# A two-layer hybrid decoder trunk on one core: padding the SBUF tiles to multiples of 256 bytes

## Chip, cores and metric

The kernel runs on one core of one Trainium2 chip. The metric is the device time of one execution in microseconds (us). Three runs of the kernel before took 1142.94, 1142.59 and 1142.89 us; the median is 1142.89.

## What is computed

One sequence of 512 tokens with 1024 channels (float32) goes through two layers, each with an RMS norm, an input projection, two mixers with SiLU gates, an output projection and a residual add; a last RMS norm follows. Cut to its shape:

```
def even_layer(x, ...):
    z = rmsnorm(x, norm_g) @ w_in                       # 1024 -> 5120
    a, g_a, u, v, g_b = split(z)
    y_a = multiscale_pool(a, pool_w, pool_scale) * silu(g_a)   # windows 2, 4, 8, 16, then a 256x256 map
    y_b = u * (tril(W_s) @ v + b) * silu(g_b)                  # in chunks of 128 tokens
    return x + concat(y_a, y_b) @ w_out                 # 2048 -> 1024
def odd_layer(x, ...):
    z = rmsnorm(x, norm_g) @ w_in                       # 1024 -> 14336
    y_c = dilated attention, 3 groups x 8 heads, merged by softmax denominators, * silu(g_c)
    y_d = d_b * conv3(d_c * d_x) * silu(g_d)
    return x + concat(y_c, y_d) @ w_out
out = rmsnorm(odd_layer(even_layer(x)))
```

## The kernel before

**Three matmuls for one product.** A float32 operand is split into a high part (rounded to the type float32r by ScalarE, `weights`, line 74, or `split`, line 81) and a low part (what is left, by VectorE, lines 75 and 82). A product is then the sum of three float32r matmuls, `mm3` (lines 85 to 88): high by high (L86), high by low (L87), low by high (L88). A matmul reads two operands from SBUF: the stationary one, which a LDWEIGHTS loads into TensorE ahead of it (128 columns), and the moving one, which streams past it (512 or 256 columns). The call `T.matmul(acc, a, b)` has `a` stationary and `b` moving.

**Where the matmuls come from.** Each of these is a loop over pieces of 1 MB of weights, loaded by SyncE (SP) into one of three `raw` buffers and split into one of two `wh` and `wl` buffers:
- `project` (line 138): two tiles of 128 output channels over all 512 tokens, 8 contraction steps x 3 matmuls each, so 48 matmuls of 512 columns a call. The weights are stationary, the normed activations `hth` and `htl` move. It is called 16 times in the even layer (names a, ga, u, gb in the trace) and 44 times in the odd one (gc 4, q 24, dc, dx, db, gd 4 each): 2880 matmuls.
- `v_half` (line 185): 2 halves x 4 token tiles x 8 steps x 3 = 192 matmuls of 512 columns. Here the activations are stationary and the weights move (name v).
- `values.near` and `values.far` (line 323 on): the same roles for the attention's values, name v too: 384 matmuls of 256 columns, and 384 of 512 columns whose stationary operand takes every fourth token (`hth[:, kk, r:S:4]`).
- `mixer_a.mix` (line 264): 48 matmuls of 512 columns, pool weights stationary (name mx).
- `out_proj` (line 150): 384 matmuls of 512 columns in each layer; the split mixer outputs `yh` and `yl` are stationary, the weights move (names eo and oo).
- In plain float32, two trace rows each: the scores (s, L399, L404), the attention's output (oa, ob; L472, L478), the chunk gate (mb, L282). The transposes (tx, L117; tp, L455, L458) take one row.

**Order of work around an attention head.** `attend` issues a head's scores; then the softmax runs on VectorE, ScalarE and GpSimd, while TensorE goes on with the next projections. `after(3, ...)` puts the head's transposes behind three more half projections (3 x 24 matmuls), `after(5, ...)` its output matmuls behind five.

**Memory.** Pools of tiles stand one behind the other in each SBUF partition: `cp` (constants, `hth`, `htl`, `y`), `wp` (`raw`, `wh`, `wl`, and the `yh`, `yl` of `out_proj`), `sp`, and then `ep` in the even layer or `ap` in the odd one. Tiles stand in the order in which they are asked for, each rounded up to 32 bytes in a partition. Ahead of `cp` lie a scratch area of 16,384 bytes and four constants of 32 bytes each, so `cp` begins 128 bytes past a multiple of 256.

Of the kernel before, what the change touches and what calls it, by code (L numbers as in the profile page):

```python
# [9 lines left out]
F32 = mybir.dt.float32  # L10
# [5 lines left out]
P = 128  # L16
S = 512
# [13 lines left out]
def trunk(ctx, tc, x, w_even, w_eout, pool_w, ws_t, bs, par, g_even, w_odd, w_oout, g_odd, g_fin, cst, out):  # L31
    nc = tc.nc
    V, A, G, T = nc.vector, nc.scalar, nc.gpsimd, nc.tensor

    cp = ctx.enter_context(tc.tile_pool(name="cp", bufs=1))
    wp = ctx.enter_context(tc.tile_pool(name="wp", bufs=2))
    sp = ctx.enter_context(tc.tile_pool(name="sp", bufs=2))
# [2 lines left out]
    def bank(name):  # L40
        return ps.tile([P, S], F32, tag="ps", name=name)

# [1 line left out]
    xt = cp.tile([P, TT, D], F32, name="xt")  # L44
    cs = cp.tile([P, 656], F32, name="cs")
    pr = cp.tile([P, 32], F32, name="pr")
    wt = cp.tile([P, 4, P], F32, name="wt")
    bsb = cp.tile([P, 4, P], F32, name="bsb")
    hth = cp.tile([P, KT, S], FR, name="hth")
# [8 lines left out]
        nc.sync.dma_start(t, src.partition_broadcast(P))  # L58
        return t

    eps = cp.tile([P, 2], F32, name="eps")
    V.memset(eps, EPS)
    A.activation(eps[:, 1:2], eps[:, 0:1], AF.Sqrt)

# [1 line left out]
    def weights(src, name, pieces=1):  # L66
        raw = wp.tile([P, CH], F32, tag="raw", name="r" + name, bufs=3)
        hi = wp.tile([P, CH], FR, tag="wh", name="h" + name, bufs=2)
        lo = wp.tile([P, CH], FR, tag="wl", name="l" + name, bufs=2)
        n = CH // pieces  # L70
        for i in range(pieces):
            at = slice(i * n, (i + 1) * n)
            nc.sync.dma_start(raw[:, at], src[:, at])
            A.activation(hi[:, at], raw[:, at], AF.Copy)  # L74
            V.tensor_sub(lo[:, at], raw[:, at], hi[:, at].bitcast(F32))  # L75
        return hi, lo
# [10 lines left out]
        T.matmul(acc, ah, bl, start=False, stop=False)  # L87
        T.matmul(acc, al, bh, start=False, stop=last)  # L88

# [1 line left out]
    def normed(tt, g, name, acc=None, then=None):  # L91
        o = sp.tile([P, D], F32, tag="xn", name=name, bufs=2)
        st = sp.tile([P, 6], F32, tag="st", name="st" + name, bufs=4)
        for h in range(2):
            xs = xt[:, tt, h * S:(h + 1) * S]
            if acc:
                V.tensor_add(xs, acc[h], xs)
            A.activation(o[:, h * S:(h + 1) * S], xs, AF.Square, accum_out=st[:, h:h + 1])
        ss, m, rt, u = (st[:, i:i + 1] for i in range(2, 6))
        V.tensor_add(ss, st[:, 0:1], st[:, 1:2])  # L100
        A.activation(rt, ss, AF.Sqrt, scale=1.0 / D, bias=eps[:, 0:1])
        V.tensor_scalar(m, ss, -0.5 / D, -0.5 * EPS, op0=ALU.mult, op1=ALU.add)
        V.reciprocal(rt, rt)
        V.scalar_tensor_tensor(u, rt, m, rt, op0=ALU.mult, op1=ALU.mult)
        V.scalar_tensor_tensor(u, u, 1.5, rt, op0=ALU.add, op1=ALU.mult)
        for h in range(2):
            at = slice(h * S, (h + 1) * S)
            V.scalar_tensor_tensor(o[:, at], xt[:, tt, at], u, g[:, at], op0=ALU.mult, op1=ALU.mult)
            if then:
                then(h, o[:, at])  # L110
        return o
# [9 lines left out]
            A.activation(dh, bv, AF.Copy)  # L121
            V.tensor_sub(dl, bv, dh.bitcast(F32))  # L122

# [1 line left out]
    pending = []  # L125

    def after(n, work):
        pending.append([n, work])
# [5 lines left out]
                pending.remove(item)  # L134
                item[1]()

# [1 line left out]
    def project(src, name, use):  # L138
        wh, wl = weights(src, name)
        wh = wh.rearrange("p (j k c) -> p j k c", j=2, k=KT)  # L140
        wl = wl.rearrange("p (j k c) -> p j k c", j=2, k=KT)
        for j in range(2):
            acc = bank(f"{name}_{j}")
            for k in range(KT):
                mm3(acc, wh[:, j, k, :], wl[:, j, k, :], hth[:, k, :], htl[:, k, :], k == 0, k == KT - 1)
            use(j, acc)
            tick()

# [1 line left out]
    def out_proj(src, name, last):  # L150
        acc = [[bank(f"{name}{t}{h}") for h in range(2)] for t in range(TT)]
        parts = {}

        def load(c):
            wh, wl = weights(src[c], f"{name}w{c}")
            parts[c] = (wh.rearrange("p (k d) -> p k d", k=2), wl.rearrange("p (k d) -> p k d", k=2),
                        *split(y[c], wp, "y", f"{name}y{c}"))

        def step(c, t, halves=(0, 1)):
            wh, wl, yh, yl = parts[c]  # L160
            tok = slice(t * P, (t + 1) * P)
            for h in halves:
                cols = slice(h * S, (h + 1) * S)
                for k in range(2):
                    mm3(acc[t][h], yh[:, k, tok], yl[:, k, tok], wh[:, k, cols], wl[:, k, cols],
                        c == 0 and k == 0, c == 7 and k == 1)

        for c in range(6):
            load(c)
            for t in range(TT):  # L170
                step(c, t)
        load(6)
        load(7)
        last(step, acc)

    # ================= even layer =================
    for h in range(2):
        nc.sync.dma_start(xt[:, 0, h * S:(h + 1) * S], x[0:P, h * S:(h + 1) * S])
    nc.sync.dma_start(ident, cst[:, 0:P])
# [1 line left out]

    with ExitStack() as ec:
        ep = ec.enter_context(tc.tile_pool(name="ep", bufs=2))

        def v_half(c):
            vb = ep.tile([P, TT, S], F32, tag="vb", name=f"vb{c}", bufs=1)
# [54 lines left out]

        def mixer_a(g):
            w = 2 << g
            pwr = ep.tile([P, 2, 16 + S], F32, tag="sum", name=f"pwr{g}")[:, :, 0:256]
            nc.sync.dma_start(pwr, pool_w[g].rearrange("p (c d) -> p c d", c=2))
            pwh, pwl = split(pwr, ep, "pw", f"pw{g}", bufs=1)
            ab = ep.tile([P, 2, 16 + S], F32, tag="ab", name=f"ab{g}", bufs=1)
            V.memset(ab[:, :, 0:16], 0.0)
            project(w_even[4 + 4 * g], f"a{g}", lambda j, acc: A.activation(ab[:, j, 16:], acc, AF.Copy))
            cur = ab  # L250
            for k in range(g + 1):
                sh, lo = 1 << k, (2 << k) - 1
                nxt = ep.tile([P, 2, 16 + S], F32, tag="sum", name=f"sum{g}{k}")
                V.tensor_add(nxt[:, :, lo:], cur[:, :, lo:], cur[:, :, lo - sh:16 + S - sh])
                cur = nxt
            pl = ep.tile([P, 2, 16 + S], F32, tag="sum", name=f"pl{g}")[:, :, 16:]
            V.scalar_tensor_tensor(pl, cur[:, :, 16:], 1.0 / w, ab[:, :, 16:], op0=ALU.mult, op1=ALU.subtract)
            V.tensor_mul(cur[:, :, 16:16 + w - 1], cur[:, :, 16:16 + w - 1],
                         inv[:, None, 0:w - 1].to_broadcast([P, 2, w - 1]))
            V.tensor_sub(pl[:, :, 0:w - 1], cur[:, :, 16:16 + w - 1], ab[:, :, 16:16 + w - 1])  # L260
            plh, pll = split(pl, ep, "pl", f"pl{g}", bufs=1)
            sg = gate(w_even[5 + 4 * g], f"ga{g}")

            def mix():
                for d in range(2):
                    acc = bank(f"mx{g}{d}")
                    dc = slice(d * P, (d + 1) * P)
                    for c in range(2):
                        mm3(acc, pwh[:, c, dc], pwl[:, c, dc], plh[:, c, :], pll[:, c, :], c == 0, c == 1)
                    V.scalar_tensor_tensor(y[g][:, d, :], acc, pr[:, 2 * g + d:2 * g + d + 1], sg[:, d, :],  # L270
                                           op0=ALU.mult, op1=ALU.mult)

            after(2, mix)
# [40 lines left out]

    out_proj(w_eout, "eo", into_odd)

    # ================= odd layer =================
    slopes = [2.0 ** (-8.0 * (n + 1) / (SLOTS * N_DIL)) for n in range(SLOTS * N_DIL)]
    with ExitStack() as oc:
        ap = oc.enter_context(tc.tile_pool(name="ap", bufs=2))  # L320

        # values, token-major, for two heads: group 0 in the order of the tokens, groups 1 and 2 by residue
        def values(p):
            v0 = ap.tile([P, 4, 256], F32, tag="v0", name=f"v0{p}", bufs=1)
            v12 = ap.tile([P, 4, 512], F32, tag="v12", name=f"v12{p}", bufs=1)
# [57 lines left out]
                project(w_odd[10 * (h // 2) + 4 + 3 * (h % 2) + g], f"q{h}{g}", use)  # L383
            return qk

        # columns of the scores of group 0: query block 0 has one block of keys, the others two
        g0c = [(0, 0, 128), (0, 128, 384), (1, 0, 256), (1, 256, 512)]
        sc = [y[4 + i // 2][:, i % 2, :] for i in range(4)]
        pt = [y[6 + i // 2][:, i % 2, :] for i in range(4)]
# [1 line left out]
        def attend(h, qk, v0, v12):  # L391
# [28 lines left out]
            blocks += [(g, r, sc[1 + g][:, r * P:(r + 1) * P]) for g in (1, 2) for r in range(4)]  # L420
            for g, n, v in blocks:
                A.activation(v, v, AF.Exp, bias=nm[:, g, n:n + 1], accum_out=ls[:, g, n:n + 1])
            # ---- merge of the groups: statistics of groups 1 and 2 in the order of group 0
            mn = ap.tile([P, 3, 4], F32, tag="mn", name=f"mn{h}")
            ml = ap.tile([P, 3, 4], F32, tag="ml", name=f"ml{h}")
            G.tensor_copy(mn[:, 0, :], nm[:, 0, :])
# [66 lines left out]
            for h in (2 * p, 2 * p + 1):  # L493
                attend(h, queries(h), v0, v12)

        # ---- short gated convolution
        for c in range(4):
            dc, cv, zz = ([ap.tile([P, S + 2], F32, tag=f"qk{2 * i + j}", name=f"{n}{c}{j}", bufs=1) for j in range(2)]
                          for i, n in enumerate(("dc", "cv", "zz")))
# [46 lines left out]


def _columns(w, starts):
    """[chunk, partition, (tile, k, column)]: chunks of two tiles of 128 columns."""
    t = np.stack([w[:, s:s + P] for s in starts])  # L550
    t = t.reshape(len(starts) // 2, 2, KT, P, P)
    return np.ascontiguousarray(t.transpose(0, 3, 1, 2, 4)).reshape(-1, P, CH)
# [61 lines left out]
```

## Time and profile before

| | |
|---|---|
| median of 3 runs | 1142.89 us |
| profiled execution, first to last instruction (span) | 1141.2 us |
| PE busy | 1123.6 us, 98% of the span |
| PEld (weight loads) | 944.5 us, 83% |
| VectorE, ScalarE, GpSimd busy | 452.1, 357.6, 142.5 us |
| mean DMA rate | 92 GB/s |

The profile gives no time of this execution other than its span, which is 1.7 us under the median. In the profile PE is TensorE's matmul row and PEld its weight loads, DVE is VectorE, ACT ScalarE, POOL GpSimd, SP the DMA queue of SyncE. Matmuls overlap: a row's duration is longer than the distance from one matmul's start to the next, and that distance is what a matmul costs in a stream of them. It is read from the starts in the timeline; a matmul's mean duration in the table of groups moves with it.

### The profile page before, as it was taken

The numbers are of one execution on the slowest core, as the hardware profiler recorded it, in microseconds if no ns is written. First come the engines' busy times: TensorE is split into PE (matmuls) and PEld (weight loads), VectorE is DVE, ScalarE is ACT, GpSimd is POOL, SyncE is SP. The second block draws the span as 40 slices with busy tenths as digits, with TensorE's granted clock in tenths as the row PEclk, the third lists the DMA queues.
The fourth block names the chain that finished last, engine by engine and source line by source line (L and its number), as shares of the span: only waits on it lengthen the run. The fifth ranks groups of instructions, "written<-read, shape, count | busy, mean of one in ns | idle before, by whom it ended". The sixth has DMA issues, their size and how long they took to land.

```text
span 1141.2 us, 12809 instructions
## 1 busy us (share of the span) xinstructions
PE 1123.6 (98%) x5288; PEld 944.5 (83%) x5288; DVE 452.1 (40%) x617; ACT 357.6 (31%) x532; POOL 142.5 (12%) x460
## 2 busy tenths in 40 slices
PE   6999999999999999999999999999999999999997
PEld 4788888888888988898889988898888888888885
DVE  6344315342255225433345225432345341432326
ACT  5323223222245214432424324332423222121323
POOL 0001000101000004320224004220124011011000
PEclk9999999999999999999999999999999999999999
DMA  9232232222323231222222221222221222323211
GB/s 333 85 111 83 74 110 83 94 91 74 111 74 120 84 111 53 95 74 76 106 79 71 77 104 50 106 74 75 85 100 51 97 88 97 109 77 111 74 37 74
DMA packets 18282, 104.98 MB, mean 92 GB/s; under 512 B 2096, under 2 KB 3248, under 8 KB 6704
## 3 DMA queue, kind: packets, MB, share of 16 engines
q1 hardware_dynamic: 18224, 104.17, 26.1%
q8 instruction: 41, 0.67, 0.2%
q14 instruction: 17, 0.14, 0.0%
HBM read 102.06 MB, written 2.10 MB: 91 GB/s over the span
## 4 chain that ended last, share of the span: by engine, by line
PE 98%; DMA 1%; ACT 0%; SPq 0%; DVE 0%; issue 0%; DVEq 0%
PE q L88 8%; PE q L87 8%; PE q L86 8%; PE v L86 5%; PE v L88 5%; PE v L87 5%; PE eo L86 3%; PE oo L86 3%; PE eo L87 3%; PE oo L88 3%; PE oo L87 3%; PE eo L88 3%; PE gc L86 1%; PE gd L86 1%; PE dx L86 1%; PE db L86 1%
## 5 line engine op out<-in xcount | busy, mean ns | idle before, releaser
L86 PE MATMUL q<-hth,hq 128*128 128x512 f32 x384 | 152.9, 398 | 0.0
L88 PE MATMUL q<-hth,lq 128*128 128x512 f32 x384 | 152.0, 396 | 0.0
L87 PE MATMUL q<-htl,hq 128*128 128x512 f32 x384 | 151.9, 395 | 0.0
L86 PE MATMUL v<-hv,hth 128*128 128x512 f32 (+1 forms) x320 | 114.6, 358 | 0.6 <-ACT hth L121 0.6
L87 PE MATMUL v<-lv,hth 128*128 128x512 f32 (+1 forms) x320 | 112.5, 352 | 0.2 <-DVE lv L75 0.2
L88 PE MATMUL v<-hv,htl 128*128 128x512 f32 (+1 forms) x320 | 112.5, 352 | 0.0
L88 PEld LDWEIGHTS q<-hth,lq 128*128 128x128 f32 x384 | 72.1, 188 | 17.4
L87 PEld LDWEIGHTS q<-htl,hq 128*128 128x128 f32 x384 | 72.2, 188 | 16.8
L86 PEld LDWEIGHTS q<-hth,hq 128*128 128x128 f32 x384 | 72.2, 188 | 16.6
L86 PEld LDWEIGHTS v<-hv,hth 128*128 128x128 f32 x320 | 76.0, 237 | 4.9 <-ACT hth L121 1.9
L87 PEld LDWEIGHTS v<-lv,hth 128*128 128x128 f32 x320 | 76.2, 238 | 3.8 <-DVE lv L75 0.9
L88 PEld LDWEIGHTS v<-hv,htl 128*128 128x128 f32 x320 | 75.9, 237 | 3.3 <-DVE htl L122 0.6
L75 DVE TENSOR_TENSOR lq<-rq,hq 128x2048 fp32r<-128x2048 f32 x24 | 54.9, 2289 | 50.7 <-ACT hq L74 50.7
L74 ACT ACTIVATE hq<-rq 128x2048 fp32r<-128x2048 f32 x24 | 45.9, 1914 | 79.6 <-PE q L87 57.2
L75 DVE TENSOR_TENSOR lv<-rv,hv 128x2048 fp32r<-128x2048 f32 (+1 forms) x22 | 37.4, 1705 | 40.5 <-ACT hv L74 40.5
L87 PE MATMUL eo<-leow,heoy 128*128 128x512 f32 x128 | 49.9, 390 | 0.0
L88 PE MATMUL eo<-heow,leoy 128*128 128x512 f32 x128 | 49.9, 390 | 0.0
L86 PE MATMUL eo<-heow,heoy 128*128 128x512 f32 x128 | 49.8, 391 | 0.0
L87 PE MATMUL oo<-loow,hooy 128*128 128x512 f32 x128 | 49.7, 390 | 0.0
L88 PE MATMUL oo<-hoow,looy 128*128 128x512 f32 x128 | 49.7, 389 | 0.0
L74 ACT ACTIVATE hv<-rv 128x2048 fp32r<-128x2048 f32 (+1 forms) x22 | 31.6, 1445 | 57.4 <-PE v L88 17.1
L86 PE MATMUL oo<-hoow,hooy 128*128 128x512 f32 x128 | 49.5, 390 | 0.0
(218 smaller groups left out, 2179.4 us busy)
## 6 DMA issues: line engine op xcount, KB each, us to landing
rq<-in_w_odd SPq DMA_DIRECT2D x24, 1024.0 KB, 4.7
rv<-in_w_odd SPq DMA_DIRECT2D x12, 1024.0 KB, 4.7
reow<-in_w_eout SPq DMA_DIRECT2D x8, 1024.0 KB, 4.7
roow<-in_w_oout SPq DMA_DIRECT2D x8, 1024.0 KB, 4.8
ra<-in_w_even SPq DMA_DIRECT2D x4, 1024.0 KB, 4.7
rga<-in_w_even SPq DMA_DIRECT2D x4, 1024.0 KB, 4.8
ru<-in_w_even SPq DMA_DIRECT2D x4, 1024.0 KB, 4.8
rgb<-in_w_even SPq DMA_DIRECT2D x4, 1024.0 KB, 4.7
```

Of the source, the lines that this page charges most:

```text
L74: A.activation(hi[:, at], raw[:, at], AF.Copy)
L75: V.tensor_sub(lo[:, at], raw[:, at], hi[:, at].bitcast(F32))
L86: T.matmul(acc, ah, bh, start=first, stop=False)
L87: T.matmul(acc, ah, bl, start=False, stop=False)
L88: T.matmul(acc, al, bh, start=False, stop=last)
```

## The change

Tiles whose size was no multiple of 256 bytes are asked for larger, and the part used is cut out of them: `cs` (2624 to 2816 bytes in a partition), `pr` (128 to 256), `eps` (8 to 256), `st` of `normed` (24 to 256) and the tiles of `mixer_a` (4224 to 4352, by a helper `padded`). The scratch area at the start of SBUF goes from 16,384 to 4,096 bytes. Comment lines become empty lines, and line numbers behind them move by up to 6.

```
-    cs = cp.tile([P, 656], F32, name="cs")
-    pr = cp.tile([P, 32], F32, name="pr")
+    cs = cp.tile([P, 704], F32, name="cs")[:, 0:656]
+    pr = cp.tile([P, 64], F32, name="pr")[:, 0:32]
...
-    eps = cp.tile([P, 2], F32, name="eps")
+    eps = cp.tile([P, 64], F32, name="eps")[:, 0:2]
...
-        st = sp.tile([P, 6], F32, tag="st", name="st" + name, bufs=4)
+        st = sp.tile([P, 64], F32, tag="st", name="st" + name, bufs=4)
...
+        def padded(name, tag="sum", bufs=2):
+            t = ep.tile([P, 1088], F32, tag=tag, name=name, bufs=bufs)
+            return t[:, 0:2 * (16 + S)].rearrange("p (c t) -> p c t", c=2)
...
-            pwr = ep.tile([P, 2, 16 + S], F32, tag="sum", name=f"pwr{g}")[:, :, 0:256]
+            pwr = padded(f"pwr{g}")[:, :, 0:256]
...
-            ab = ep.tile([P, 2, 16 + S], F32, tag="ab", name=f"ab{g}", bufs=1)
+            ab = padded(f"ab{g}", "ab", 1)
...
-                nxt = ep.tile([P, 2, 16 + S], F32, tag="sum", name=f"sum{g}{k}")
+                nxt = padded(f"sum{g}{k}")
...
-            pl = ep.tile([P, 2, 16 + S], F32, tag="sum", name=f"pl{g}")[:, :, 16:]
+            pl = padded(f"pl{g}")[:, :, 16:]
...
-    nc = _bacc.Bacc("TRN2", target_bir_lowering=False, num_devices=1)
+    nc = _bacc.Bacc("TRN2", target_bir_lowering=False, num_devices=1, dynamic_dma_scratch_size=4096)
```

The instructions and their order on every engine are the same in both programs; only addresses differ. Start addresses in the two built programs, modulo 256 (every slice that a matmul takes begins a multiple of 256 bytes behind its tile's start, but for the strided ones of `far`, which begin 4r bytes behind it, r = 0 to 3):

| matmuls | stationary, moving before | moving less stationary, before | after |
|---|---|---|---|
| project (2880) | wh, wl 96; hth, htl 64 | 224 | 0 |
| v_half (192), near (384) | hth, htl 64; wh, wl 96 | 32 | 0 |
| far (384) | hth, htl 64 + 4r; wh, wl 96 | 32 - 4r | 0, 252, 248, 244 |
| mx (48) | pool weights 224; pooled values 96 | 128 | 0 |
| out_proj (768) | yh, yl 96; wh, wl 96 | 0 | 0 |
| ob, oa, mb | v, vb 224; y, wt 64 | 96 | 0 |
| tp; tx | y 64; xa, xb 96; ident 128 | 64; 32 | 0 |
| s (`qk` tiles of 2056 bytes, 2080 apart) | one slot apart | 32 | 32 |

The `qk` tiles of the odd layer are not padded. Modulo 512, the two operands of `out_proj` have the same address too, before and after; those of `project`, `v_half` and `near` differ by 256 after the change.

## Rows read from the trace of the kernel before

**Rows 1.** The page: engines' busy time, and the chain that ended last.
```profile
PE 1123.6 (98%) x5288; PEld 944.5 (83%) x5288; DVE 452.1 (40%) x617; ACT 357.6 (31%) x532; POOL 142.5 (12%) x460
...
PE 98%; DMA 1%; ACT 0%; SPq 0%; DVE 0%; issue 0%; DVEq 0%
```
**Rows 2.** Groups of PE instructions by form: names, shapes, count, busy us, mean ns, idle before.
```profile
L88 PE MATMUL q<-hth,lq 128*128 128x512 f32 x384 | 152.0, 396 | 0.0
...
L88 PE MATMUL v<-hv,htl 128*128 128x512 f32 x192 | 76.8, 401 | 0.0
...
L88 PE MATMUL eo<-heow,leoy 128*128 128x512 f32 x128 | 49.9, 390 | 0.0
...
L88 PE MATMUL oo<-hoow,looy 128*128 128x512 f32 x128 | 49.7, 389 | 0.0
...
L478 PE MATMUL ob<-y,v 128*128 128x128 f32 x128 | 15.6, 275 | 0.0
...
L458 PE MATMUL tp<-cs,y 128*128 128x128 f32 x64 | 8.3, 273 | 0.0
```
**Rows 3.** Timeline of PE (start us, us), out_proj: first and last of 48 matmuls.
```profile
270.12 0.39 PE L86 MATMUL eo<-heow,heoy 128*128 128x512 f32 x1
...
280.77 0.39 PE L88 MATMUL eo<-heow,leoy 128*128 128x512 f32 x1
```
**Rows 4.** Timeline of PE, v_half of the second half: first and last of 96 matmuls.
```profile
138.11 0.39 PE L86 MATMUL v<-hv,hth 128*128 128x512 f32 x1
...
160.28 0.39 PE L88 MATMUL v<-hv,htl 128*128 128x512 f32 x1
```
**Rows 5.** Timeline of PE, three calls of project: first and last of 144 matmuls.
```profile
396.28 0.39 PE L86 MATMUL q<-hth,hq 128*128 128x512 f32 x1
...
429.64 0.39 PE L88 MATMUL q<-hth,lq 128*128 128x512 f32 x1
```
**Rows 6.** Busy time by stretch, eo twice, then v: PE, PEld, DVE, ACT, POOL, PEclk, DMA.
```profile
270.12:275.33 5.21, 5.21 (x24) 4.32 (x23) 3.52 (x2) 2.85 (x2) 0.00 (x0) 1.00 0.00 0
275.33:280.77 5.44, 5.44 (x25) 4.51 (x24) 0.00 (x0) 0.00 (x0) 0.00 (x0) 1.00 0.57 193
...
144.64:149.54 4.90, 4.90 (x22) 3.94 (x21) 0.00 (x0) 0.00 (x0) 0.00 (x0) 1.00 0.37 155
```
**Rows 7.** Timeline of PE, mx: first and last of 12 matmuls.
```profile
74.78 0.39 PE L86 MATMUL mx<-hpl,hpw 128*128 128x512 f32 x1
...
77.33 0.39 PE L88 MATMUL mx<-hpl,lpw 128*128 128x512 f32 x1
```
**Rows 8.** Timeline of PE, out_proj: its first and seventh matmul; 23 behind a stall.
```profile
259.22 0.39 PE L86 MATMUL eo<-heow,heoy 128*128 128x512 f32 x1
...
260.60 0.39 PE L86 MATMUL eo<-heow,heoy 128*128 128x512 f32 x1
...
1115.27 0.40 PE L87 MATMUL oo<-loow,hooy 128*128 128x512 f32 x1
...
1120.37 0.62 PE L88 MATMUL oo<-hoow,looy 128*128 128x512 f32 x2
```
**Rows 9.** Timeline of PE, near (256 columns): first and last of 96 matmuls.
```profile
514.07 0.28 PE L86 MATMUL v<-hv,hth 128*128 128x256 f32 x1
...
525.26 0.29 PE L88 MATMUL v<-hv,htl 128*128 128x256 f32 x1
```
**Rows 10.** Timeline of PE, far (strided stationary operand): first and last of 96 matmuls.
```profile
373.57 0.40 PE L86 MATMUL v<-hv,hth 128*128 128x512 f32 x1
...
396.04 0.40 PE L88 MATMUL v<-hv,htl 128*128 128x512 f32 x1
```
**Rows 11.** Timeline of DVE and PEld, first head: last softmax scalings, loads of the transposes.
```profile
449.91 1.07 DVE L446 TENSOR_SCALAR y<-y,ff 128x128 f32<-128x128 f32 x5 [0.63 <-POOL ff L444]
...
450.62 0.91 PEld L458 LDWEIGHTS tp<-cs,y 128*128 128x128 f32 x8
```
**Rows 12.** The page: one of the DMA issues (KB each, us to landing).
```profile
rq<-in_w_odd SPq DMA_DIRECT2D x24, 1024.0 KB, 4.7
```

## The prediction

> **What bounds the kernel now.** I read the page's totals first, then the chain that ended last, then the groups of matmuls by form, then the timeline of PE. TensorE bounds it: PE is busy for 98% of the span and holds 98% of the chain; VectorE, the busiest of the others, stands at 40% [rows 1]. So only what a stream of matmuls costs per matmul can move the end by much.
>
> The groups show that matmuls of one form do not cost the same: 128x512 takes 396 ns in project (q), 401 in v (strided ones among them), but 390 and 389 in the two output projections [rows 2]. The distance between starts is what counts. In out_proj 48 matmuls start from 270.12 to 280.77: 10.65 us / 47 = **226.6 ns** [rows 3]. In v_half 96 start from 138.11 to 160.28: 22.17 / 95 = **233.4 ns** [rows 4]. In project 144 start from 396.28 to 429.64: 33.36 / 143 = **233.3 ns** [rows 5].
>
> What makes 6.7 ns? [...] Not the other engines or the DMA either: out_proj keeps its rhythm both in a stretch in which DVE is busy 3.52 of 5.21 us, ACT 2.85 and the DMA not at all, and in the next one with DVE and ACT idle and the DMA at 0.57 (23 and 24 steps, 226.5 and 226.7 ns); v_half keeps its own with all three other engines idle (21 steps in 4.90 us, 233.3) [rows 6]. Not the roles of the operands: project has weights stationary, v_half has them moving, and both cost the same. v_half and out_proj have the same roles, shapes and `mm3`. What is left is where the operands lie: in out_proj both begin at the same address modulo 256 (and modulo 512), in v_half and project they are 32 bytes off, one way or the other. The mx matmuls, 128 off, are no better: 12 start from 74.78 to 77.33, 2.55 / 11 = 232 ns [rows 7].
>
> The better rhythm is not there at once. The first seven matmuls of out_proj start 1.38 / 6 = 230 ns apart, and after the stall in the second one 23 start 5.10 / 22 = 232 ns apart [rows 8]. So a stream with equal addresses settles into it, and loses it at a break; the streams 32 off never settle, not in 143 steps.
>
> **The change, part by part.** No instruction is added, removed or reordered. Five costs:
>
> 1. *Contiguous matmuls of 512 columns in project, v_half and mx*, 2880 + 192 + 48 = 3120, go from 32 or 128 off to 0. I take out_proj's rhythm for them: 3120 x (233.3 - 226.6 = 6.7 ns) = -20.9 us. Bounds: nothing, if addresses are not the cause or if equality modulo 256 is not enough; -20.9 us in full.
>
> 2. *Breaks.* Score, transpose, output and gate matmuls, far's strided ones and short stalls cut these streams. Of the first, eight heads give 24 breaks, the eight mixers of the even layer 4 by the gate matmuls (mx is itself of the settled kind), far 4; with hiccups like the one behind [rows 8] I reckon 60. What a break costs: out_proj's start loses 6 x (230 - 226.6) = 20 ns, the stall's 22 steps lose 22 x (231.8 - 226.6) = 114 ns. Most look like the first, so 40 ns each: +2.4 us; bounds +1.2 and +6.8 us.
>
> 3. *near*, 384 matmuls of 256 columns, 32 off: 96 start from 514.07 to 525.26, 11.19 / 95 = 117.8 ns [rows 9]. With 233.3 at 512 columns that is 0.451 ns a column and 2.3 ns fixed. With 226.6 at 512 and the same fixed part it is 0.438 a column, 114.4 ns at 256: 384 x 3.4 = -1.3 us; bounds 0 and -2.6 (if the whole 6.7 ns came off each).
>
> 4. *far*, 384 strided: 22.47 / 95 = 236.5 ns [rows 10]. The trace holds them at 32, 28, 24 and 20 off, and afterwards only a quarter is at 0. No equal strided pair shows in the trace. I take nothing, by these rows themselves, in which the offset of r changes nothing over 96 matmuls; ends: -3.8 us if they reached 226.6, +1 us (3 ns each, what striding costs against [rows 4]) if they lose.
>
> 5. *Plain float32*: ob, oa and mb go from 96 off to 0, tp from 64. ob takes 275 ns, tp 273 [rows 2]; I give the 208 rows of 128 columns of ob, oa, mb those 2 ns: -0.4 us, ends 0 and -0.8. The scores stay 32 off: nothing.
>
> *Cover that gets thin.* Between a head's scores and its transposes lie 72 projection matmuls; they shrink by up to 72 x 6.7 = 0.48 us, while the softmax does not. In the first head the last scaling ends at 449.91 + 1.07 = 450.98, and the last of eight transposes' loads, 0.91 us from 450.62 less one load of 0.14, starts at 451.39: 0.41 us to spare [rows 11]. So TensorE would be 0.07 us late there; eight heads alike would give 0.6 us, one alone 0.1, and I add +0.1 us. VectorE, 60% idle [rows 1], has room to split the weights earlier.
>
> *Padding and scratch.* No instruction handles the added bytes. [...]
>
> Sum: -20.9 + 2.4 - 1.3 - 0.4 + 0.1 = **-20.1 us**. The profiled execution spans 1141.2 us, so 1121.1; the median of the runs is 1.7 above that span, so **1122.8 us**.
>
> [...] Rows 3 to 5 show streams whose only difference is the operands' place, 6.7 ns apart; that gives the -20.1 above. [...]
>
> **The rivals.**
>
> *No change* (0.13, 1142 us). Two ways lead there. The rhythm of out_proj may come from something that I took for the same, as its order over eight accumulators instead of one; then project stays at 233.3 ns. Or addresses count modulo 512: every pair in out_proj is equal modulo 512 too, and no pair in the trace is 256 off, while project's will be. Then step 1 is 0 and only a few tenths of a us come from float32. For it: 128 off is as bad as 32 off [rows 7]. Against: 128 off shows that halving the distance is not what counts, but nothing rules 512 out.
>
> *It settles late* (0.12, 1130 us). Each break costs what the stall in [rows 8] cost, and streams between breaks are short: 60 x 22 x 5.2 ns = 6.9 us instead of 2.4, and near, in runs of 96, gains nothing: 1122.8 + 4.5 + 1.3 = 1128.6; with 40 breaks more, 1133.
>
> *Slower* (0.04, 1153 us). Reads that begin in step at the same place could hold each other up in project, where the activations move past; the price is that of the strided far stream, the slowest here, 236.5 against 233.3 [rows 5, 10]: 3120 x 3.2 = +10 us. It decides if project's starts come more than 233.3 ns apart. Against it: out_proj is in step already, and is the fastest.
>
> **How the numbers follow.** The forecast has 0.71: every stream of the trace with equal addresses has the short rhythm and every one without has the long. Its own range runs from 1117 (far gains 3.8, breaks cost 1.2 instead of 2.4, near 1.3 more) to 1127 (breaks at 6.8). With the late settling the range 1117 to 1132 holds 0.83. Under 1140.6 counts as faster, over 1145.2 as slower (0.2% is 2.3 us, about what runs of this kernel can tell from no change): faster 0.71 + 0.12 = 0.83, same 0.13, slower 0.04.
>
> **What would show it.** Right: starts in q, dc, ga and u about 226.6 ns apart within a few matmuls after each break, their mean duration down from 396 to 390 ns, out_proj unchanged, near at 114 to 115 ns, far still about 236.5, the scores unchanged. Step 1 is wrong if q still starts every 233.3 ns; step 2 if the short rhythm comes only after tens of matmuls; the slack if DVE L446 shows up among what the transposes wait for. A gain of over 27 us would mean that equal addresses give more than out_proj's rows hold.

## The result, and the profile after

The changed kernel took **1124.35 us** (median; 1123.55 to 1124.62) against 1142.74 us of the kernel before on the same chip: a ratio of 0.9839, 95% interval 0.9825 to 0.9852. That is 18.4 us less; 1122.8 was predicted, in a range of 1117 to 1132. The span of the profiled execution went from 1141.2 to 1122.9 us.

The page of the changed kernel, its totals and the chain, answers to [rows 1]:

```profile
PE 1105.0 (98%) x5288; PEld 945.4 (84%) x5288; DVE 452.0 (40%) x617; ACT 357.5 (32%) x532; POOL 142.6 (13%) x460
...
PE 98%; DMA 1%; ACT 0%; DVE 0%; SPq 0%; issue 0%; DVEq 0%
```

PE lost 18.6 us of busy time and still holds 98% of the chain; the others are within 0.9 us of what they were. So the gain is in the matmuls themselves. Groups of its PE instructions by form, to be held against [rows 2] (L88 to L90 were L86 to L88):

```profile
L90 PE MATMUL q<-hth,lq 128*128 128x512 f32 x384 | 149.6, 389 | 0.0
...
L90 PE MATMUL eo<-heow,leoy 128*128 128x512 f32 x128 | 49.9, 390 | 0.0
L90 PE MATMUL oo<-hoow,looy 128*128 128x512 f32 x128 | 49.7, 389 | 0.0
...
L90 PE MATMUL v<-hv,htl 128*128 128x256 f32 x128 | 36.2, 283 | 0.0
...
L464 PE MATMUL tp<-cs,y 128*128 128x128 f32 x64 | 8.3, 273 | 0.0
```

Near's row (v, 256 columns) before the change:

```profile
L88 PE MATMUL v<-hv,htl 128*128 128x256 f32 x128 | 35.7, 279 | 0.0
```

Project's matmuls came down from 396 to 389 ns, to where out_proj's were and still are; near's of 256 columns went up, from 279 to 283; the transposes stayed. The timeline of PE gives the distances of starts: the first and last of 144 matmuls of project, then of 96 of near:

```profile
390.59 0.40 PE L88 MATMUL q<-hth,hq 128*128 128x512 f32 x1
...
423.01 0.39 PE L90 MATMUL q<-hth,lq 128*128 128x512 f32 x1
...
506.27 0.28 PE L88 MATMUL v<-hv,hth 128*128 128x256 f32 x1
...
517.65 0.28 PE L90 MATMUL v<-hv,htl 128*128 128x256 f32 x1
```

32.42 / 143 = 226.7 ns for project (233.3 in [rows 5]) and 11.38 / 95 = 119.8 ns for near (117.8 in [rows 9]). Summed over all starts of each kind, the change from before to after is:

| matmuls | before, us | after, us | difference | predicted |
|---|---|---|---|---|
| project (2880) | 673.7 | 655.7 | -17.9 | |
| v_half (192) | 47.2 | 46.7 | -0.5 | |
| mx (48) | 11.2 | 10.9 | -0.3 | |
| these three together | | | -18.7 | -20.9 + 2.4 = -18.5 |
| near (384) | 45.3 | 46.1 | +0.9 | -1.3 |
| far (384) | 92.1 | 91.5 | -0.6 | 0 |
| plain float32: ob, oa, mb | | | 0.0 | -0.4 |
| out_proj (768) | 174.6 | 174.6 | 0.0 | 0 |
| transposes (tp) | 12.44 | 12.48 | +0.04 | +0.1 |

-18.7 + 0.9 - 0.6 = -18.4 us is the whole of the gain.

### The profile page after: what moved, and what is told of

The parts are those of the page before. It is cut to its first block, busy times and chain, and to the rows that moved or that the text cites. A ratio compares the mean times of both kernels' runs of the same rounds, so it can differ in the third digit from the quotient of the medians.

```text
span 1122.9 us, 12809 instructions
## 1 busy us (share of the span) xinstructions
PE 1105.0 (98%) x5288; PEld 945.4 (84%) x5288; DVE 452.0 (40%) x617; ACT 357.5 (32%) x532; POOL 142.6 (13%) x460
## 4 chain that ended last, share of the span: by engine, by line
PE 98%; DMA 1%; ACT 0%; DVE 0%; SPq 0%; issue 0%; DVEq 0%
PE q L90 8%; PE q L88 8%; PE q L89 8%; PE v L88 6%; PE v L90 5%; PE v L89 5%; PE oo L88 3%; PE eo L90 3%; PE eo L88 3%; PE oo L90 3%; PE eo L89 3%; PE oo L89 3%; PE gc L88 1%; PE gc L89 1%; PE gc L90 1%; PE dx L90 1%
## 5 line engine op out<-in xcount | busy, mean ns | idle before, releaser
L88 PE MATMUL q<-hth,hq 128*128 128x512 f32 x384 | 150.5, 392 | 0.0
L90 PE MATMUL q<-hth,lq 128*128 128x512 f32 x384 | 149.6, 389 | 0.0
L89 PE MATMUL q<-htl,hq 128*128 128x512 f32 x384 | 149.5, 389 | 0.0
L88 PE MATMUL v<-hv,hth 128*128 128x512 f32 (+1 forms) x320 | 114.8, 359 | 0.9 <-ACT hth L123 0.9
L90 PE MATMUL v<-hv,htl 128*128 128x512 f32 (+1 forms) x320 | 112.8, 353 | 0.0
L89 PE MATMUL v<-lv,hth 128*128 128x512 f32 (+1 forms) x320 | 112.6, 352 | 0.0
L90 PEld LDWEIGHTS q<-hth,lq 128*128 128x128 f32 x384 | 72.1, 188 | 15.1
L89 PEld LDWEIGHTS q<-htl,hq 128*128 128x128 f32 x384 | 72.1, 188 | 14.6
L88 PEld LDWEIGHTS q<-hth,hq 128*128 128x128 f32 x384 | 72.2, 188 | 14.4
L88 PEld LDWEIGHTS v<-hv,hth 128*128 128x128 f32 x320 | 76.6, 239 | 4.7 <-ACT hth L123 2.1
L90 PEld LDWEIGHTS v<-hv,htl 128*128 128x128 f32 x320 | 76.5, 239 | 3.2 <-DVE htl L124 0.7
L89 PEld LDWEIGHTS v<-lv,hth 128*128 128x128 f32 x320 | 76.8, 240 | 2.7
L90 PE MATMUL eo<-heow,leoy 128*128 128x512 f32 x128 | 49.9, 390 | 0.0
L89 PE MATMUL eo<-leow,heoy 128*128 128x512 f32 x128 | 49.8, 389 | 0.0
L88 PE MATMUL eo<-heow,heoy 128*128 128x512 f32 x128 | 49.8, 392 | 0.0
L89 PE MATMUL oo<-loow,hooy 128*128 128x512 f32 x128 | 49.7, 389 | 0.0
L90 PE MATMUL oo<-hoow,looy 128*128 128x512 f32 x128 | 49.7, 389 | 0.0
L88 PE MATMUL oo<-hoow,hooy 128*128 128x512 f32 x128 | 49.5, 390 | 0.0
```

The source lines that it names most:

```text
L88: T.matmul(acc, ah, bh, start=first, stop=False)
```

## The experiments

Two theories stood against each other. **A**: what counts is whether the two operands of a matmul have the same address modulo 256. **B**: it is something else that the change altered (the absolute place, the scratch area, the padding). Distances of starts below are means from the timeline with those over 300 ns left out; before the change project had 233.3 by this measure, out_proj 227.1, near 117.9, and after it 227.0, 227.1 and 120.1.

**One edit of the change alone, in the kernel before.**

```
-    eps = cp.tile([P, 2], F32, name="eps")
+    eps = cp.tile([P, 64], F32, name="eps")[:, 0:2]
```

> The kernel before with one edit of the change alone: `eps` is asked for with 256 bytes instead of 8. That moves `wp` to 64 modulo 256, where `hth` and `htl` lie already; scratch, `cs`, `pr`, `st` and the tiles of `mixer_a` stay as they were, and mx stays 128 off. Theory A (what counts is that the two operands of a matmul have the same address modulo 256): project and v_half go to 226.7 ns from start to start, mx stays at 232 to 233, near goes from 117.8 to 120.0 as in the changed kernel; 1124.6 us, within 1 us of the change. Theory B (what counts is the absolute place: both at 128, the smaller scratch area, or the padding as such): project stays at 233.3 ns and the time at 1142.7 us.

Measured: 1124.28 us (1124.08 to 1124.80), ratio 0.9834, interval 0.9819 to 0.9849. Project 227.0 ns, mx 233.0, near 120.1. By form, where mx stays slow beside a fast project:

```profile
L88 PE MATMUL q<-hth,lq 128*128 128x512 f32 x384 | 149.6, 390 | 0.0
...
L88 PE MATMUL mx<-hpl,lpw 128*128 128x512 f32 x16 | 6.3, 394 | 0.0
```

So this one line is the whole change, but for 0.3 us of mx. The smaller scratch area and the other padded tiles, which this run leaves out, add nothing by themselves (1124.28 against 1124.35 us); in the changed kernel, which has them, the loads of q's weights land in 4.7 us as in [rows 12]. B falls as far as it named those.

**The same edit undone in the changed kernel.**

```
-    eps = cp.tile([P, 64], F32, name="eps")[:, 0:2]
+    eps = cp.tile([P, 2], F32, name="eps")
```

> The changed kernel with this one edit undone: `eps` with 8 bytes again, so that `wp` and all behind it move by 32 against `hth`, `htl`, `y` and `wt`. Theory A: project and v_half are back at 233.3 ns, out_proj and mx (both operands in the moved part) stay at 226.7, near is back at 117.8; 1142.2 us, that is, the whole gain gone but for mx. Theory B: project keeps 226.7 ns, 1124.4 us.

Measured: 1142.62 us, ratio 0.9995, interval 0.9985 to 1.0004. Project 233.3 ns, out_proj 227.1, mx 227.1, near 117.9, all as A had it:

```profile
L90 PE MATMUL mx<-hpl,lpw 128*128 128x512 f32 x16 | 6.2, 389 | 0.0
...
L90 PE MATMUL q<-hth,lq 128*128 128x512 f32 x384 | 151.9, 396 | 0.0
```

**Everything moved by 32 bytes together.**

```
-    pr = cp.tile([P, 64], F32, name="pr")[:, 0:32]
+    pr = cp.tile([P, 72], F32, name="pr")[:, 0:32]
```

> The changed kernel with `pr` 32 bytes larger: `hth`, `htl`, `wt`, `y` and everything in `wp`, `sp` and `ep` now begin at 160 modulo 256, no longer at 128, with equal addresses as in the change; only the transposes' `ident` is 32 off. Theory A: all as in the change, 226.7 ns in project, 1124.4 us. Theory B (128 itself matters): project goes back to 233 ns and 1142 us.

Measured: 1124.01 us, ratio 0.9831, interval 0.9811 to 0.9850; project 227.0 ns.

```profile
L90 PE MATMUL q<-hth,lq 128*128 128x512 f32 x384 | 149.6, 390 | 0.0
```

The step of 32 bytes in the absolute address made no difference (227.0 ns in project with it and without); B is gone. That the tiles are whole multiples of 256 bytes is not the point either, only that operands come to stand alike.

**Other distances between `wp` and the activations.** `eps` of 96 or 80 elements puts `wp` 128 or 64 bytes further:

```
-    eps = cp.tile([P, 64], F32, name="eps")[:, 0:2]
+    eps = cp.tile([P, 96], F32, name="eps")[:, 0:2]
```

> The changed kernel with `eps` of 384 bytes: `wp` lies 128 past `hth` and `htl` modulo 256. Theory A with the number 256: project and v_half are at 232 to 233 ns (as mx was before, whose runs were only 24 matmuls long), out_proj and mx at 226.7; 1142 us. Rival C (128 bytes apart is as good as equal, and mx was only too short to settle): project at 226.7 ns and 1124.4 us. For near nothing is known at 128: between 114 and 122 ns.

> The changed kernel with `eps` of 320 bytes: `wp` lies 64 past `hth` and `htl`, so project is at 192 and v_half and near at 64 modulo 256. Theory A (equal modulo 256, nothing less): project and v_half at 232 to 233.5 ns, 1142 us, out_proj at 226.7. Rival C in a weaker form (a multiple of 64 will do): excluded by the run 128 off already, where project stood at 232.7, unless 64 and 192 are kinder than 128; then 226.7 and 1124.4 us. Near: 117.9 at 32, 119.2 at 128 and 120.1 at 0 leave 117.5 to 119.5 for 64.

Measured: 128 off 1142.61 us (ratio 0.9994, 0.9984 to 1.0004), 64 off 1144.29 us (1.0013, 1.0002 to 1.0025); project 232.7 and 233.3 ns, out_proj 227.0 in both runs, near 119.2 and 118.1. (Far, 236.6 before the change and 235.0 after it, rose to 239.3 and 239.6.) By form, first 128 off, then 64 off:

```profile
L90 PE MATMUL eo<-heow,leoy 128*128 128x512 f32 x128 | 49.8, 389 | 0.0
...
L90 PE MATMUL q<-hth,lq 128*128 128x512 f32 x384 | 151.5, 395 | 0.0
```

```profile
L90 PE MATMUL eo<-heow,leoy 128*128 128x512 f32 x128 | 49.9, 390 | 0.0
...
L90 PE MATMUL q<-hth,lq 128*128 128x512 f32 x384 | 151.6, 395 | 0.0
```

Rival C falls: even streams of over 100 matmuls do not come to 226.7 at 64 or 128 off, as they do not at 32. And the changed kernel itself answers the question of 512: project's operands are 256 apart modulo 512 there, out_proj's are equal, and both run at 226.7 ns once settled.

**Sixteen and four bytes off.** Tiles are rounded to 32 bytes, slices are not:

```
-        hi = wp.tile([P, CH], FR, tag="wh", name="h" + name, bufs=2)
-        lo = wp.tile([P, CH], FR, tag="wl", name="l" + name, bufs=2)
+        hi = wp.tile([P, CH + 64], FR, tag="wh", name="h" + name, bufs=2)[:, 4:4 + CH]
+        lo = wp.tile([P, CH + 64], FR, tag="wl", name="l" + name, bufs=2)[:, 4:4 + CH]
```

(with 1 in place of 4 for four bytes).

> The changed kernel with `wh` and `wl` 256 bytes larger and the weights 16 bytes behind their start: project is 16 off one way, v_half, near and both out_proj 16 off the other way; mx stays equal. Theory A in its strict form (equal and nothing near it): project, v_half and out_proj all leave 226.7 for 230 to 234 ns; with out_proj's 768 as well that is 1142.4 + 768 x 6.4 ns = 1147 us. Rival D (anything within 32 bytes of equal is as good): all stay at 226.7 ns, 1124.4 us.

> As the run 16 off, with the weights 4 bytes, one element, behind the start of their tile. Strict form of theory A: 230 to 234 ns in project, v_half and out_proj, 1147 us. Rival D in a narrower form (the same 16 bytes will do): 226.7 ns, 1124.4 us. That the strided stream's parts at 4, 8 and 12 bytes less than equal cost about what its part at 0 cost in the changed kernel speaks neither way, since striding has its own rhythm.

Measured: 16 off 1137.74 us (0.9957, 0.9938 to 0.9977), 4 off 1150.61 us (1.0069, 1.0046 to 1.0092). Rival D falls: four bytes spoil it, with project at 232.4 ns and out_proj at 236.7. At 4 bytes the strict form of A holds in its direction, and its numbers need mending. At 16 bytes it holds for out_proj (231.8 ns throughout) but not for all of project, whose mean of 231.0 hides two rhythms: every stretch without a break ran near 226.7 or near 233.3 ns once it had settled, at one and the same offset. Two of them, first and last of 144 matmuls each, from the timeline of PE 16 off:

```profile
393.04 0.40 PE L88 MATMUL q<-hth,hq 128*128 128x512 f32 x1
...
426.41 0.40 PE L90 MATMUL q<-hth,lq 128*128 128x512 f32 x1
...
521.67 0.40 PE L88 MATMUL q<-hth,hq 128*128 128x512 f32 x1
...
554.09 0.39 PE L90 MATMUL q<-hth,lq 128*128 128x512 f32 x1
```

33.37 / 143 = 233.4 ns and 32.42 / 143 = 226.7 ns. About a third of project's matmuls had the short rhythm: all four stretches that follow mx and all four that follow near, but none of the 18 that follow an attention head's scores, transposes or output matmuls, one of them 647 matmuls long. So equal addresses are not the only ones that allow the short rhythm: 16 off it depends on what the stream meets at its start, and with equal addresses every stream of project came to it. Why a start decides is not shown. The run came out 9 us under its expectation, most of it this third of project (some 1000 x 6.6 ns) and near, which fell to 114.8 ns, the lowest of all runs. By form, 16 off, then 4 off:

```profile
L90 PE MATMUL eo<-heow,leoy 128*128 128x512 f32 x128 | 50.4, 394 | 0.0
...
L90 PE MATMUL v<-hv,htl 128*128 128x256 f32 x128 | 35.4, 277 | 0.0
```

```profile
L90 PE MATMUL eo<-heow,leoy 128*128 128x512 f32 x128 | 51.1, 399 | 0.0
...
L90 PE MATMUL v<-hv,htl 128*128 128x256 f32 x128 | 36.8, 287 | 0.0
```

**One of the three matmuls off.** Does each matmul pay for itself, or does a stream keep time as a whole? Only `wl` was moved, by 32 bytes:

```
-        lo = wp.tile([P, CH], FR, tag="wl", name="l" + name, bufs=2)
+        lo = wp.tile([P, CH + 64], FR, tag="wl", name="l" + name, bufs=2)[:, 8:8 + CH]
```

> The changed kernel with only the low parts of the weights, `wl`, 32 bytes off; `wh`, `hth`, `htl`, `yh` and `yl` stay equal. One of the three matmuls of each `mm3` in project (L90, stationary), v_half and out_proj (L89, moving) is off, two are equal. Pairwise reading (each matmul, or each load beside a stream, has its own price): one in three at 233.3 and two at 226.7, 228.9 ns on average; 3840 x 2.2 = +8.4, 1132.8 us. Reading by rhythm (a stream settles only if all its members are in step): all three at about 233, 3840 x 6.5 = +25, 1149 us.

Measured: 1146.42 us, ratio 1.0028 (1.0017 to 1.0040); project 233.2 ns, out_proj 233.1. The reading by rhythm holds: with two of three still in step the mean is that of streams wholly out of step. (It is 2.6 us under the 1149 expected; near, which nobody had put in, gave 1.0 of that with 117.5 ns.) Within the three the cost is not even:

```profile
L88 PE MATMUL q<-hth,hq 128*128 128x512 f32 x384 | 152.6, 397 | 0.0
...
L89 PE MATMUL q<-htl,hq 128*128 128x512 f32 x384 | 153.4, 399 | 0.0
...
L90 PE MATMUL q<-hth,lq 128*128 128x512 f32 x384 | 149.5, 389 | 0.0
```

L90 is the one whose own stationary operand is off, and it is the shortest. L89, the matmul ahead of it, is the longest: in q 238.5 ns pass on average from its start to L90's, 228.2 from L90's to L88's. L90's weights are loaded while L89 streams, as one triple in the trace of the changed kernel has it: L89 starts at 401.02 us, L90 at 401.25, and that load takes 0.19 us from 401.03. So the rows point to the load of the next matmul and the stream of this one as the pair that has to be in step. That this is the mechanism is argued, not shown, and it is not the whole of it: from L88's start to L89's, with all operands of both equal, 232.6 ns pass too.

**A version with near 16 bytes off and the rest equal**, next to the changed kernel once more on the same chip:

```
-    def weights(src, name, pieces=1):
+    def weights(src, name, pieces=1, off=0):
...
+        hi = wp.tile([P, CH + 64], FR, tag="wh", name="h" + name, bufs=2)[:, off:off + CH]
+        lo = wp.tile([P, CH + 64], FR, tag="wl", name="l" + name, bufs=2)[:, off:off + CH]
...
-                wh, wl = weights(w_odd[10 * p], f"v0{p}")
+                wh, wl = weights(w_odd[10 * p], f"v0{p}", off=4)
```

> The changed kernel with the weights of `near` alone 16 bytes behind equal (their tiles 256 bytes larger, the slice begins at 16 bytes); everything else equal as in the change. In the run 16 off near had 114.8 ns a matmul instead of 120.1. If each stream answers to its own offset alone: near at 114.8, project, v_half and out_proj at 226.7 to 227.0, and 384 x 5.3 ns = 2.0 us less than the change, 1122.3 us. If the offset of one stream spoils the rhythm of the next (it begins anew behind each near): up to 4 x 23 matmuls at 232, 0.5 us of it lost again.

> The changed kernel itself, on the same chip as the two others, for the comparison: 1124.4 us, project at 227.0 ns, near at 120.1.

Measured: 1122.96 us (1122.72 to 1123.19; ratio to before 0.9823, 0.9809 to 0.9836) against 1123.82 us (1123.37 to 1124.30; 0.9830, 0.9817 to 0.9844) of the change: 0.9 us better, no run of one among those of the other, the fastest version of this study. But near stands at 117.4 ns, not at 114.8; project stayed at 227.0:

```profile
L90 PE MATMUL v<-hv,htl 128*128 128x256 f32 x128 | 35.7, 279 | 0.0
```

Half of the expected 2.0 us came, and the expectation was wrong in its first form: near's own offset does not settle its time. At the same 16 bytes three of its four passes ran at 113.4 ns where all weights were 16 off, and at 116.6 here. As in project 16 off, what it meets when it begins seems to choose between the two; why was not tried.

## Why the prediction was right

**The cause.** The argument was by exclusion: two kinds of streams with the same shapes, roles and neighbours at 226.6 and 233.4 ns [rows 3, 4], at a granted clock of 1.00, in busy and quiet stretches alike [rows 6], so the place of the operands is left. The runs with `eps` alone, with `eps` undone and with all moved together (227.0, 233.3 and 227.0 ns in project) show directly that the place of one operand against the other sets the distance. The rival "no change" had two legs. That out_proj's rhythm comes from its order is gone, since project reached it; that 512 is the number is gone, since 256 apart is as good (226.7 ns). "Slower" is gone with project's 226.7 ns, and "it settles late" with what breaks cost, below. The gain is 18.4 us, and four bytes of address make 10 ns a matmul in out_proj (227.1 to 236.7). By what means an address makes this difference, no run shows.

**Steps 1 and 2.** Together -18.5 us predicted, -18.7 measured; the cause was right, and that the sum is so close is partly luck, by errors that cancel. Breaks were dear in the forecast: 60 at 40 ns, 2.4 us. In project the mean is 227.0 against 226.67 settled, and 2880 x 0.29 ns = 0.8 us, 1.6 less. Against that, v_half gained 0.8 less than its part of the 20.9, and project some 0.6 less: before the change its mean was 233.25 and not 233.3, and 23 distances of over 300 ns behind other matmuls did not shrink. One such break in the changed kernel, the timeline of PE behind a head's scores:

```profile
426.46 0.48 PE L88 MATMUL q<-hth,hq 128*128 128x512 f32 x1
...
428.63 0.39 PE L88 MATMUL q<-hth,hq 128*128 128x512 f32 x1
...
429.99 0.39 PE L88 MATMUL q<-hth,hq 128*128 128x512 f32 x1
```

From the second matmul on the starts are some 231 ns apart until 428.63; from there six take 1.36 us, 226.7 each. Most breaks cost 20 to 40 ns, as out_proj's start did [rows 8], none in project as much as the stall there, and there are about 30, not 60: the short gate and mx streams hardly break the rhythm (project loses 10 ns at most behind one, with distances over 300 ns left out). What was not foreseen is that v_half gained 0.5 us and not 1.3. Its second half gained the 0.64 us that 6.7 ns make of 96 matmuls (22.40 to 21.76); its first half gained nothing. The kernel's first matmuls start 0.4 to 0.6 us apart for a while, four of them in the profile before and ten in the one after, at a granted clock that the profile gives as 1.00. The timeline of PE after, and behind it before:

```profile
11.99 0.63 PE L89 MATMUL v<-lv,hth 128*128 128x512 f32 x1
...
15.41 0.56 PE L88 MATMUL v<-hv,hth 128*128 128x512 f32 x1
15.81 0.39 PE L89 MATMUL v<-lv,hth 128*128 128x512 f32 x1
```

```profile
11.76 0.63 PE L87 MATMUL v<-lv,hth 128*128 128x512 f32 x1
...
12.62 0.56 PE L86 MATMUL v<-hv,hth 128*128 128x512 f32 x1
13.01 0.40 PE L87 MATMUL v<-lv,hth 128*128 128x512 f32 x1
```

This varies from run to run and is not the change: v_half took 46.1 us in the changed kernel's other profile, and 46.0 and 45.9 in the runs with `eps` alone and with all moved. What ends the slow start is not shown.

**Step 3, near, had the wrong sign**: -1.3 us forecast, +0.9 measured, outside its bounds of 0 to -2.6. These 2.2 us are more than the 1.5 us by which the time missed the forecast. The step that failed is the split of a matmul's time into a fixed part and a price per column, and the carrying over of the price from 512 columns to 256. The runs give near's distance by offset as 123.5 ns (4 bytes), 114.8 or 117.4 (16), 117.9 (32), 118.1 (64), 119.2 (128) and 120.1 (0): equal addresses are among its worst. Near's stream of 256 columns has by these runs its own order of good and bad places, and nothing in the trace of before said which; the bound should have reached above nothing.

**Step 4**, far: -0.6 us, within -3.8 and +1; it stands at 235.0 ns in all its passes, 236.6 before, and comes to 226.7 in none. The offset moves this stream too (239 to 240 ns in the runs 128 and 64 off), which the forecast had put at nothing. **Step 5**: nothing, where 0.4 was expected; that tp's 273 ns are better than ob's 275 [rows 2] has nothing to do with the offset, which went to 0 for both.

**The thin cover** was foreseen for the right head. In the changed kernel the first head's last scaling ends at 443.29 + 1.07 = 444.36, and the eight loads of the transposes, which took 0.91 us in [rows 11], take 0.98. DVE's timeline, then PEld's:

```profile
443.29 1.07 DVE L452 TENSOR_SCALAR y<-y,ff 128x128 f32<-128x128 f32 x5 [0.63 <-POOL ff L450]
```

```profile
443.57 0.98 PEld L464 LDWEIGHTS tp<-cs,y 128*128 128x128 f32 x8
```

The last load is the 0.07 us late that was forecast, once; in the other seven heads the loads take as long as before. To the hundredth that is luck: undelayed, the last load would have started at 443.57 + 0.91 - 0.14 = 444.34, only 0.02 us before the scaling ends, and it starts some 0.05 behind that end. The matmuls lose less, 0.04 us over all transposes in the table above. A further gain in project would find no cover left in that head.

## What to carry to other kernels

In a stream that is TensorE's throughout, compare the distances of starts between groups of the same shape; a few ns between them, with everything else equal, were the addresses of the operands here (233.3 against 226.7 ns), and one 256-byte tile in place of an 8-byte one gave 1.7% (the run with `eps` alone). Offsets of small tiles reach far: what stands behind `eps` moved with it. Find the good offset for each shape by a scan, and look at each stretch of a stream and not only at its mean: in these runs the rhythm took several matmuls to settle (nine behind the head's scores shown above), one member of three out of step brought the mean of all to 233.2 ns, and 16 bytes off stretches of the same kind ran at either of two rhythms, 226.7 or 233.3 ns.

## What was not expected

- Four bytes are enough to lose the short rhythm, and less is not milder: 4 bytes made the 512-column stream of out_proj slower (236.7 ns) than 16 (231.8), and 32, 64 and 128 left project between 232.7 and 233.3.
- 16 bytes off, project ran at 226.7 ns in a third of its matmuls and at 233.3 in the rest, by stretch.
- Near's streams of 256 columns had other good offsets than those of 512: 114.8 ns at 16 bytes and 120.1 at 0, where project has 231.0 and 227.0. Near also showed two rhythms at one offset (113.4 and 116.6 ns).
- The loss was the whole stream's: with `wl` moved by 32 bytes, one of three operands off brought all three to a mean of 233 ns.
